# A fp32 trunk of two layers on one core: first loads cut in pieces and spread over two queues, zeros multiplied at the start, the pooling matrices outside the weight stream, and new distances in the list scheduler

## The chip, the cores and the metric

The kernel runs on one core of a Trainium2 chip. The metric is device time in microseconds, the median of several executions; below, one further execution taken by the hardware profiler is read. Engines: TensorE (PE, with PEld for its weight loads), VectorE (DVE), ScalarE (ACT), GpSimd (POOL) and SyncE (SP), whose queue issues the DMAs.

## What is computed

The reference is a causal trunk of two layers over 512 tokens of width 1024, all in float32. Each layer normalizes, projects once, and merges three mixers:

```python
h = rms_norm(x, norm_g[l])
p = h @ w_in[l]
(cb, cc, cx, cgate, q, k, v, agate, iq, ik, iw, pu, pgate, mgate) = split_columns(p)
y_a = short_conv_mixer(cb, cc, cx, cgate, ...)            # 3-tap causal convolution, gated
y_b = sparse_attention_mixer(q, k, v, agate, iq, ik, iw, ...)  # indexer scores, top-128 keys, softmax over them, 8 heads
y_c = pool_mixer(pu, pgate, pool_w[l], pool_scale[l], ...) # causal means of 2/4/8/16 tokens minus the token, times pool_w per group
g = sigmoid(mgate)                                         # three gates of width 1024
x = x + (g[0] * y_a + g[1] * y_b + g[2] * y_c) @ w_o[l]
```

The indexer scores of a query select the 128 highest keys; the softmax runs over those alone.

## The kernel before

The stream x is held transposed: eight slices `k` of 128 features by 512 tokens. Every matrix product is made of three matmuls in a reduced float32 format (`mm3`, L393): each operand is split into a high and a low part, and high x high, high x low and low x high are accumulated in PSUM. The split (`split`, L398) is a ScalarE copy for the high part and a VectorE subtraction for the low part. A 128-column group of a projection (`project`, L456) is 24 matmuls of 512 columns.

All weights come as one stream of chunks of 128 x 1024 (`wst`), 90 per layer. `prep` (L362) loads a chunk into `raw` (2 buffers), and splits it into `whi` and `wlo` (3 buffers each); `take` (L375) hands out the next one and prepares two more ahead. Chunk 0 is loaded and split in four pieces, chunks 1 and 2 in two, all others whole. One chunk of the stream, `pw`, is half empty and holds the pooling matrices; it is taken ahead of the pooling loop (L615) and its buffers stay in use until the fourth group is mixed (`mix`, L643).

At the start, SP issues all loads in turn: the vectors `vt`, the eight slices of x, and pieces of the first three chunks among them. `load_x` (L415) makes of each slice the scaled high and low parts `xhi` and `xlo` and a square, which POOL sums into `ss`. The first projections are a `wavefront` (L464) of three chunks over the slices as they arrive: `ps_ik`, `pa0`, `pb0`. Later come the indexer's scores (`select`, L556) and 16 rounds of `max` and `match_replace` for each of three token blocks (L576, L577), the pooling mixer, its merge (L591), the q and k projections of one quad of heads, v, attention for that quad (scores of a head and block in a bank `sc` of which there are 2; L724 is the first step of the softmax, on VectorE), the convolution, the second quad, and two more merges; `w_o` and the residual end the layer.

The order in which instructions stand on each engine is not that of the code. `Order` (L30) reads the recorded instructions and their dependences and plays them through a list scheduler with a cost for each (`cost`, L108); the first ready instruction of the highest priority is placed, four passes are made, and the best one's order on each engine is fixed. An instruction is ready for TensorE a distance `TO_PE` after the end of what it reads; a buffer comes free a distance `LAT` after the end of its last use:

```python
LAT = {"PE": 0.2, "DVE": 0.13, "Activation": 0.14, "Pool": 0.1, "SP": 0.13}
TO_PE = {"PE": 0.003, "DVE": 0.255, "Activation": 0.27, "Pool": 0.2, "SP": 0.27}

def lat(self, a, b):
    return self.TO_PE[a] if b == "PE" else self.LAT[a]
```

These numbers only set the order; on the chip an engine waits for what an instruction needs and for nothing else.

Of the kernel before, what the change touches and what calls it, by code (L numbers as in the profile page):

```python
# [5 lines left out]
F32 = mybir.dt.float32  # L6
F32R = mybir.dt.float32r
AF = mybir.ActivationFunctionType
# [3 lines left out]
LAG = 3  # L12
PASSES = 4
P = 128
S = 512
D = 1024
KT = D // P
DEPTH = 2
NCHUNK = 70 + 3 * 4 + 8
EPS = 1e-6  # L20
# [9 lines left out]
class Order:  # L30
# [6 lines left out]
    LAT = {"PE": 0.2, "DVE": 0.13, "Activation": 0.14, "Pool": 0.1, "SP": 0.13}  # L37
    TO_PE = {"PE": 0.003, "DVE": 0.255, "Activation": 0.27, "Pool": 0.2, "SP": 0.27}

# [68 lines left out]
    def cost(self, inst, kind):  # L108
# [14 lines left out]
        if kind == "InstMatmult":  # L123
            f32 = str(aps[0].dtype).endswith("float32")
            c = (0.0004167 * n + 0.003) * ((4 if n > 128 else 2) if f32 else 1)
            return c, 0.0
# [5 lines left out]
        if engine == "Pool":  # L132
            return (0.1 if kind == "InstMemset" else 0.1 + 0.0022 * n), 0.0
        if kind in ("InstMax", "InstMatchReplace"):
            return 0.069 + 0.00104 * max(size(a) for a in aps), 0.0
        fast = kind == "InstTensorScalarPtr" and len(wide) == 1 and not psum
# [165 lines left out]
@with_exitstack  # L302
def trunk(ctx, tc, xT, wst, vecs, cst, outT):
    nc = tc.nc
# [48 lines left out]

    def load(dst, src):
        nc.sync.dma_start(dst, src)  # L355

# [5 lines left out]
    def prep(i):  # L362
        l, c = divmod(i, NCHUNK)
        raw = wp.tile([P, 1024], F32, tag="raw", name=nm("raw"), bufs=2)
        hi = wp.tile([P, 1024], F32R, tag="whi", name=nm("whi"), bufs=3)
        lo = wp.tile([P, 1024], F32R, tag="wlo", name=nm("wlo"), bufs=3)
        n = 1024 // (4 if i == 0 else 2 if i < 3 else 1)
        for j in range(0, 1024, n):
            p = slice(j, j + n)
            load(raw[:, p], wst[l, c, :, p])  # L370
            act.activation(hi[:, p], raw[:, p], AF.Copy)  # L371
            dve.tensor_tensor(out=lo[:, p], in0=raw[:, p], in1=hi[:, p].bitcast(F32), op=ALU.subtract)  # L372
        wq[i] = (hi, lo)
# [66 lines left out]


    load(vt, vecs)
    for k in range(KT):
        if k in (0, 2, 4):
            prep(state["next"])
            state["next"] += 1
        if k % 4 == 0:
            xin = big(F32)
        load(xin[:, k % 4], xT[k])
        load_x(0, k, xin[:, k % 4])  # L450
# [24 lines left out]
    for l in range(DEPTH):  # L475
# [138 lines left out]

        pwh, pwl = take()  # L615
        yh, yl = big(), big()
# [217 lines left out]
def _columns():  # L834
# [13 lines left out]
    t += ab(iq, 0) + ab(iq, 1)  # L848
    t += ["pw"]
    for i in range(4):  # L850
# [13 lines left out]
def _layout(x, norm_g, w_in, conv_w, w_out_conv, q_norm_g, k_norm_g, w_out_attn, pool_w, pool_scale, w_out_pool, w_o):  # L864
# [4 lines left out]
    for l in range(DEPTH):  # L869
# [3 lines left out]
        for t in tiles:  # L873
            if isinstance(t, str) and t == "v":
                wst[l, n] = w[:, 2 * vc:2 * vc + 2, v0:v0 + S].reshape(P, 1024)
                vc += 1
                n += 1
            elif isinstance(t, str) and t == "pw":
                wst[l, n, :, :S] = pool_w[l].transpose(1, 0, 2).reshape(P, S)
                n += 1  # L880
            elif isinstance(t, str):
                br, wo = outs[t]
                wo = wo[l].reshape(4, P, KT, P).transpose(1, 2, 0, 3)
                for d in range(KT):
                    c = mg0 + br * D + d * P
                    wst[l, n] = w[:, :, c:c + P].reshape(P, 1024)
                    n += 1
                    if d % 2 == 1:
                        wst[l, n] = wo[:, d - 1:d + 1].reshape(P, 1024)
                        n += 1  # L890
            else:
                wst[l, n].reshape(P, KT, P)[:, :, :len(t)] = w[:, :, t]
                n += 1
# [13 lines left out]
    xT = np.ascontiguousarray(x[0].T.reshape(KT, P, S))  # L907
    return xT, wst, vecs

# [34 lines left out]
```

## Time and profile before

| | us |
|---|---|
| median of 3 runs (lowest, highest) | 1079.22 (1078.21, 1079.63) |
| the profiled execution, its own time | 1078.84 |
| its span, first to last instruction | 1077.1 |
| TensorE busy | 1065.4 |
| VectorE busy | 799.2 |
| ScalarE busy | 465.5 |
| first matmul starts | 6.51 |

The span is what the trace covers; the execution's own time is 1.7 us longer. Busy time of TensorE runs from a matmul's issue to its modelled end, so that consecutive ones overlap (390 ns each, started 227 ns apart); how fast they go is read from their starts.

### The profile page before, as it was taken

To read this page: it belongs to the slowest core of one execution; us is meant where nothing else is said; L and a number is where in the kernel's file an instruction comes from. 1 tells how busy PE (TensorE), PEld (TensorE's weight loads), DVE (VectorE), ACT (ScalarE), POOL (GpSimd) and SP (SyncE) were. 2 spreads that over 40 slices of the span, in tenths; PEclk is the share of its full clock that TensorE was granted. 3 is DMA by queue.
4 is the path that set the end of the run, shared out by engine and by line. 5 is a ranking of instruction groups with operands and counts; after the bars stand their busy time and mean duration, and the time that the engine had idled before them with its cause. 6 is when DMAs were issued, how large, how long until landed. Compare 5 with 4: busy or idle time off the path is not lost.

```text
span 1077.1 us, 13444 instructions
## 1 busy us (share of the span) xinstructions
PE 1065.4 (99%) x4842; PEld 878.4 (82%) x4842; DVE 799.2 (74%) x1389; ACT 465.5 (43%) x747; POOL 97.2 (9%) x76
## 2 busy tenths in 40 slices
PE   7999999999999999999999999999999999999998
PEld 6888888888888888888888888888888878888886
DVE  6889999997558865455559899999876598744442
ACT  6355233485233673233334542235852347623320
POOL 4000000000000011221210000000000001132210
PEclk9999999999999999999999999999999999999999
DMA  6542322452234522234535322225423245122352
GB/s 226 153 140 78 99 98 94 133 152 72 82 102 130 160 75 78 98 98 164 169 117 153 115 86 98 98 79 166 128 79 98 79 144 149 61 98 98 98 195 78
DMA packets 44402, 124.39 MB, mean 115 GB/s; under 512 B 6960, under 2 KB 7472, under 8 KB 44336
## 3 DMA queue, kind: packets, MB, share of 16 engines
q1 hardware_dynamic: 44336, 123.53, 36.4%
q8 instruction: 38, 0.62, 0.2%
q14 instruction: 28, 0.23, 0.1%
HBM read 101.49 MB, written 4.19 MB: 98 GB/s over the span
## 4 chain that ended last, share of the span: by engine, by line
PE 96%; DVE 1%; DMA 1%; issue 0%; ACT 0%; SPq 0%; DVEq 0%; ACTq 0%
PE pj L388 87%; PE sc L388 4%; PE pv L388 3%; PE pt L391 2%; DMA b<-in_x 0%; DVE wlo L372 0%; DMA k<-h 0%; DVE w L488 0%; SPq L355 0%; DVE h L401 0%; ACT whi L371 0%; DVE w L649 0%; ACT xhi L403 0%; DVE w L435 0%; DVE w L436 0%
## 5 line engine op out<-in xcount | busy, mean ns | idle before, releaser
L388 PE MATMUL pj<-xhi,whi 128*128 128x512 f32 x1040 | 373.1, 393 | 6.5 <-ACT whi L371 6.5
L388 PE MATMUL pj<-xlo,whi 128*128 128x512 f32 x1040 | 372.8, 393 | 0.0
L388 PE MATMUL pj<-xhi,wlo 128*128 128x512 f32 x1040 | 372.4, 393 | 0.0
L371 ACT ACTIVATE whi<-raw 128x1024 fp32r<-128x1024 f32 (+2 forms) x185 | 191.5, 1036 | 385.6 <-PE pj L388 358.9
L372 DVE TENSOR_TENSOR wlo<-raw,whi 128x1024 fp32r<-128x1024 f32 (+2 forms) x185 | 228.5, 1239 | 15.5 <-ACT whi L371 14.8
L388 PEld LDWEIGHTS pj<-xhi,whi 128*128 128x128 f32 x1040 | 195.0, 188 | 46.7 <-ACT whi L371 6.7
L388 PEld LDWEIGHTS pj<-xhi,wlo 128*128 128x128 f32 x1040 | 195.7, 188 | 39.4 <-DVE wlo L372 0.5
L388 PEld LDWEIGHTS pj<-xlo,whi 128*128 128x128 f32 x1040 | 195.5, 188 | 39.4
L388 PE MATMUL pj<-b,whi 128*128 128x512 f32 x640 | 210.7, 390 | 0.0
L385 DVE TENSOR_TENSOR w<-pj,ss 128x512 f32<-128x512 f32 x104 | 70.8, 684 | 93.3 <-PE pj L388 93.0
L388 PEld LDWEIGHTS pj<-b,whi 128*128 128x128 f32 x640 | 120.0, 188 | 24.2
L388 PE MATMUL pj<-b,wlo 128*128 128x512 f32 x320 | 118.2, 391 | 0.0
L610 POOL TENSOR_TENSOR b<-b,w 128x512 f32<-128x512 f32 x32 | 60.6, 1899 | 264.5 <-DVE w L608 264.4
L388 PEld LDWEIGHTS pj<-b,wlo 128*128 128x128 f32 x320 | 60.1, 188 | 12.3
L576 DVE MAX8 m<-score 128x8 f32<-128x256 f32 (+2 forms) x96 | 53.2, 557 | 1.7
L577 DVE MATCH_REPLACE8 score<-m,score 128x384 f32<-128x384 f32 (+2 forms) x96 | 52.0, 542 | 0.0
L742 DVE TENSOR_TENSOR pth<-pt,pth 128x128 fp32r<-128x128 f32 (+1 forms) x64 | 31.1, 486 | 18.7 <-PE pv L388 9.4
L819 DVE TENSOR_TENSOR w<-pj,w 128x512 f32<-128x512 f32 x16 | 11.0, 690 | 44.4 <-PE pj L388 42.8
L727 ACT ACTIVATE a<-a,mn 128x128 f32<-128x128 f32 (+1 forms) x64 | 35.6, 557 | 15.5 <-DVE mn L724 14.9
L665 POOL TENSOR_TENSOR w<-w,w 128x512 f32<-128x512 f32 x8 | 11.9, 1492 | 325.4 <-ACT w L664 325.4
L388 PE MATMUL pv<-pth,b 128*128 128x512 f32 (+3 forms) x128 | 39.9, 316 | 0.0
L741 ACT ACTIVATE pth<-pt 128x128 fp32r<-128x128 f32 (+1 forms) x64 | 27.6, 432 | 27.4 <-PE pt L391 20.1
(119 smaller groups left out, 999.7 us busy)
## 6 DMA issues: line engine op xcount, KB each, us to landing
raw<-in_w SPq DMA_DIRECT2D x177, 512.0 KB, 3.3
b<-h SPq DMA_DIRECT2D x128, 64.0 KB, 2.2
k<-h SPq DMA_DIRECT2D x64, 128.0 KB, 3.2
b<-in_x SPq DMA_DIRECT2D x8, 256.0 KB, 4.8
w<-in_x SPq DMA_DIRECT2D x8, 256.0 KB, 5.5
xs<-w SPq DMA_DIRECT2D x8, 256.0 KB, 2.3
w<-xs SPq DMA_DIRECT2D x8, 256.0 KB, 3.9
out_x<-w SPq DMA_DIRECT2D x8, 256.0 KB, 2.0
```

Source lines behind the costliest of these rows:

```text
L371: act.activation(hi[:, p], raw[:, p], AF.Copy)
L372: dve.tensor_tensor(out=lo[:, p], in0=raw[:, p], in1=hi[:, p].bitcast(F32), op=ALU.subtract)
L385: dve.tensor_tensor(out=out, in0=ps, in1=by, op=ALU.mult)
L388: pe.matmul(ps, lhs, rhs, start=start, stop=stop)
L391: pe.transpose(out, src, ident if n == P else ident[64:64 + n, 64:64 + n])
L576: dve.max(m8, score)
L577: dve.match_replace(score, m8, score, -3.0e38)
L610: gp.tensor_tensor(out=a, in0=a, in1=g, op=ALU.add)
L665: gp.tensor_tensor(out=s0, in0=s0, in1=s1, op=ALU.add)
L727: act.activation(pr[:, :w], pr[:, :w], AF.Exp, bias=mn, scale=-1.0, accum_out=zs)
L741: act.activation(dh, pst[:, :b + 1, :], AF.Copy)
L742: dve.tensor_tensor(out=dl, in0=pst[:, :b + 1, :], in1=dh.bitcast(F32), op=ALU.subtract)
```

## The change

The distances and three costs of the scheduler change; the first three chunks are loaded in pieces of 128, 128, 256 and 512 columns, each directly behind the x slice that needs it first, into tiles of the pool `b`; the first x slice is issued by ScalarE's queue instead of SP's; six matmuls of a zero tile into an unused PSUM bank stand at the start; all three first chunks are there before the loop ends; and the pooling matrices have an input and a load of their own, split into a tile of the pool `b`.

```diff
+WARM = 6
-NCHUNK = 70 + 3 * 4 + 8
+NCHUNK = 69 + 3 * 4 + 8
...
-    TO_PE = {"PE": 0.003, "DVE": 0.255, "Activation": 0.27, "Pool": 0.2, "SP": 0.27}
+    TO_PE = {"PE": 0.0, "DVE": 1.2, "Activation": 1.2, "Pool": 1.2, "SP": 2.0}
...
-            c = (0.0004167 * n + 0.003) * ((4 if n > 128 else 2) if f32 else 1)
+            c = (0.000423 * n + 0.01) * ((4 if n > 128 else 2) if f32 else 1)
...
-            return (0.1 if kind == "InstMemset" else 0.1 + 0.0022 * n), 0.0
+            return (0.1 if kind == "InstMemset" else 0.1 + 0.003 * n), 0.0
         if kind in ("InstMax", "InstMatchReplace"):
-            return 0.069 + 0.00104 * max(size(a) for a in aps), 0.0
+            n = max(size(a) for a in aps)
+            return 0.069 + 0.00104 * n + 0.076 * (kind == "InstMatchReplace"), 0.0
...
-    def load(dst, src):
-        nc.sync.dma_start(dst, src)
+    def load(dst, src, queue=nc.sync):
+        queue.dma_start(dst, src)
...
-        n = 1024 // (4 if i == 0 else 2 if i < 3 else 1)
-        for j in range(0, 1024, n):
-            p = slice(j, j + n)
-            load(raw[:, p], wst[l, c, :, p])
-            act.activation(hi[:, p], raw[:, p], AF.Copy)
-            dve.tensor_tensor(out=lo[:, p], in0=raw[:, p], in1=hi[:, p].bitcast(F32), op=ALU.subtract)
+        load(raw, wst[l, c])
+        split(hi, lo, raw)
...
-    load(vt, vecs)
+    idle = W(F32R)
+    gp.memset(idle.bitcast(F32), 0.0)
+    warm = pt()
+    for n in range(WARM):
+        mm(warm.rearrange("p a b -> p (a b)"), idle[:, :P], idle, n == 0, n == WARM - 1)
+    HEAD = 3
+    raws = [big(F32).rearrange("p (a b) s -> p a (b s)", a=2) for _ in range(2)]
+    heads = []
+    for i in range(HEAD):
+        hi = wp.tile([P, 1024], F32R, tag="whi", name=nm("whi"), bufs=3)
+        lo = wp.tile([P, 1024], F32R, tag="wlo", name=nm("wlo"), bufs=3)
+        wq[i] = (hi, lo)
+        heads.append((raws[i // 2][:, i % 2], hi, lo))
+    state["next"] = HEAD
+    piece = {0: 1, 1: 1, 2: 2, 4: 4}
     for k in range(KT):
-        if k in (0, 2, 4):
-            prep(state["next"])
-            state["next"] += 1
         if k % 4 == 0:
             xin = big(F32)
-        load(xin[:, k % 4], xT[k])
+        load(xin[:, k % 4], xT[k], nc.scalar if k == 0 else nc.sync)
+        for i, (raw, hi, lo) in enumerate(heads if k in piece else ()):
+            p = slice(k * P, (k + piece[k]) * P)
+            load(raw[:, p], wst[0, i, :, p])
+            split(hi[:, p], lo[:, p], raw[:, p])
+            if k == 0 and i == 0:
+                load(vt, vecs)
         load_x(0, k, xin[:, k % 4])
...
-        pwh, pwl = take()
+        pw = big()
+        pwh, pwl = pw[:, 0], pw[:, 1]
+        pwr = W()
+        load(pwr, pws[l])
+        split(pwh, pwl, pwr)
```

The rest of the diff makes the new input `pws` and leaves the chunk `pw` out of the stream.

ScalarE at the start. Before (`whi_84` and `whi_117` are the first two chunks, `xhi_100` to `xhi_126` slices of x):

```order
L423 ACT_TABLE_LOAD
L423 ACTIVATE a_104<-b_98 128x512
L403 ACTIVATE xhi_100<-b_98,vt 128x512
L403 ACTIVATE xhi_109<-b_98,vt 128x512
L371 ACTIVATE whi_84<-raw_83 128x256
L423 ACTIVATE a_113<-b_98 128x512
L371 ACTIVATE whi_117<-raw_116 128x512
L403 ACTIVATE xhi_126<-b_98,vt 128x512
```

Now (`whi_93`, `whi_95`, `whi_97` are the first three chunks):

```order
L357 DMA b_99<-in_x 128x512
L421 ACT_TABLE_LOAD
L421 ACTIVATE a_115<-b_99 128x512
L401 ACTIVATE xhi_111<-b_99,vt 128x512
L398 ACTIVATE whi_93<-b_91 128x128
L398 ACTIVATE whi_95<-b_91 128x128
L398 ACTIVATE whi_97<-b_92 128x128
L401 ACTIVATE xhi_129<-b_99,vt 128x512
L398 ACTIVATE whi_93<-b_91 128x128
L421 ACTIVATE a_133<-b_99 128x512
L398 ACTIVATE whi_95<-b_91 128x128
```

The second slice's copy moved from ahead of the first piece of weights to behind three of them, and further on four squares (`a_133`, `a_150`, `a_158`, `a_176`) stand behind the first one and ahead of the last slice's copy. On TensorE the six matmuls of zeros come first, and then each slice of x is multiplied with all three chunks before the next, nine matmuls a slice, where before the first two chunks alternated and the third followed.

TensorE at the end of the first three chunks, now (`xhi_196` is the last slice's high part, `whi_207` and `whi_213` are the fourth and fifth chunk):

```order
L386 MATMUL pj_218<-xhi_196,wlo_94 128x512
L386 MATMUL pj_219<-xhi_196,whi_95 128x512
L386 MATMUL pj_219<-xlo_197,whi_95 128x512
L386 MATMUL pj_219<-xhi_196,wlo_96 128x512
L386 MATMUL pj_220<-xhi_196,whi_97 128x512
L386 MATMUL pj_220<-xlo_197,whi_97 128x512
L386 MATMUL pj_220<-xhi_196,wlo_98 128x512
L386 MATMUL pj_353<-xhi_111,whi_207 128x512
L386 MATMUL pj_353<-xlo_112,whi_207 128x512
L386 MATMUL pj_408<-xhi_111,whi_213 128x512
L386 MATMUL pj_408<-xlo_112,whi_213 128x512
L386 MATMUL pj_353<-xhi_111,wlo_208 128x512
```

Before, the third chunk's matmuls stood between the first chunk's last use and the fourth chunk's first:

```order
L388 MATMUL pj_198<-xhi_176,wlo_85 128x512
L388 MATMUL pj_200<-xlo_101,whi_142 128x512
L388 MATMUL pj_199<-xhi_176,whi_117 128x512
L388 MATMUL pj_200<-xhi_100,wlo_143 128x512
L388 MATMUL pj_199<-xlo_177,whi_117 128x512
L388 MATMUL pj_200<-xhi_109,whi_142 128x512
L388 MATMUL pj_199<-xhi_176,wlo_118 128x512
L388 MATMUL pj_200<-xlo_110,whi_142 128x512
L388 MATMUL pj_200<-xhi_109,wlo_143 128x512
L388 MATMUL pj_200<-xhi_126,whi_142 128x512
L388 MATMUL pj_333<-xhi_100,whi_187 128x512
L388 MATMUL pj_200<-xlo_127,whi_142 128x512
```

What moved is again the third chunk (`pj_200`): its 24 matmuls no longer stand ahead of and between the fourth chunk's.

VectorE at the first softmax of layer 1 (L576 and L577 are steps of the top-k, L724 the softmax's first step). Before, the last top-k steps stand among the first softmax operations:

```order
L385 TENSOR_TENSOR w_1944<-pj_1919,ss_106 128x512
L576 MAX m_210_874<-score_461 128x8
L724 ISA a_1988,mn_1989<-sc_1985,ct 128x128
L724 ISA mn_1989 128x1
L577 MATCH_REPLACE score_461<-m_210_874,score_461 128x512
L724 ISA a_1999,mn_2000<-sc_1996,score_459 128x256
L724 ISA mn_2000 128x1
L576 MAX m_211_877<-score_461 128x8
L724 ISA a_2010,mn_2011<-sc_2007,score_460 128x384
L724 ISA mn_2011 128x1
L577 MATCH_REPLACE score_461<-m_211_877,score_461 128x512
```

Now all of them, with the scaling of the mask (L594), the splits of v (L730) and two evictions (L383), stand ahead of the first softmax operation (L744):

```order
L593 MATCH_REPLACE score_481<-m_211_896,score_481 128x512
L730 SCALAR_TENSOR_TENSOR b_1922<-pv_1800,rcol_467,b_1922 128x8x64
L594 TENSOR_SCALAR score_481<-score_481 128x512
L399 TENSOR_TENSOR wlo_1970<-raw_1968,whi_1969 128x1024
L730 SCALAR_TENSOR_TENSOR b_1921<-pj_1798,rcol_467,b_1921 128x8x64
L730 SCALAR_TENSOR_TENSOR b_1922<-pj_1799,rcol_467,b_1922 128x8x64
L383 TENSOR_TENSOR w_1963<-pj_1938,ss_117 128x512
L383 TENSOR_TENSOR w_1999<-pj_1974,ss_117 128x512
L744 ISA a_2007,mn_2008<-sc_2004,ct 128x128
L744 ISA mn_2008 128x1
L744 ISA a_2018,mn_2019<-sc_2015,score_479 128x256
```

What moved are three steps of the top-k and the operations around them, from behind the first softmax operation to ahead of it.

## Rows read from the trace of the kernel before

**Rows 1.** The page: busy time of an engine, share of the span, instructions.
```profile
PE 1065.4 (99%) x4842; PEld 878.4 (82%) x4842; DVE 799.2 (74%) x1389; ACT 465.5 (43%) x747; POOL 97.2 (9%) x76
```

**Rows 2.** Chain that ended last, pieces: start us, us, what, number of instructions.
```profile
6.51 25.90 PE pj L388 x101
...
403.21 0.33 PE pt L391 x3
...
409.82 154.21 PE pj L388 x680
...
1073.31 0.69 DVE w L819
```

**Rows 3.** TensorE by shape: first and last 512-column group, largest 128-column one.
```profile
L388 PE MATMUL pj<-xhi,whi 128*128 128x512 f32 x1040 | 373.1, 393 | 6.5 <-ACT whi L371 6.5
...
L391 PE MATMUL pt<-ct,a 128*128 128x128 f32 x160 | 28.0, 273 | 0.2
...
L388 PE MATMUL sc<-h,wlo 128*128 128x512 f32 x8 | 3.1, 390 | 0.0
```

**Rows 4.** TensorE at the start: windows (busy, granted clock, DMA), then order of time.
```profile
9.00:11.00 2.00, 2.00 (x7) 1.00 1.03 364
...
10.52 1.05 PE L388 MATMUL pj<-xhi,whi 128*128 128x512 f32 x2
...
11.37 0.97 PE L388 MATMUL pj<-xlo,whi 128*128 128x512 f32 x2
```

**Rows 5.** TensorE in attention stretches: order of time, then one window of four.
```profile
901.10 0.63 PE L388 MATMUL pj<-b,whi 128*128 128x512 f32 x2
...
902.73 0.40 PE L388 MATMUL pj<-b,whi 128*128 128x512 f32 x1
...
205.00:265.00 60.00, 60.00 (x298) 1.00 0.41 120
```

**Rows 6.** TensorE in order of time: the three waits that are named.
```profile
361.45 0.69 PE L388 MATMUL sc<-k,b 128*128 128x128 f32 x4 [0.25 <-DMA k<-h]
...
605.38 0.39 PE L388 MATMUL sc<-b,b 128*128 128x256 f32 x1 [0.61 <-DVE w L649]
...
874.09 0.50 PE L388 MATMUL sc<-w,ob 128*128 128x512 f32 x1 [0.31 <-DVE w L401]
```

**Rows 7.** All engines in order of time: from the first load to the first matmul.
```profile
0.74 0.39 SPq L355 DMA_DIRECT2D b<-in_x  x1
...
3.44 0.63 ACT L423 ACTIVATE a<-b 128x512 f32<-128x512 f32 x1 [1.42 <-DMA b<-in_x]
...
3.97 0.70 ACT L403 ACTIVATE xhi<-b,vt 128x512 fp32r<-128x512 f32 x1
...
4.71 0.75 DVE L404 SCALAR_TENSOR_TENSOR xlo<-b,vt,xhi 128x512 fp32r<-128x512 f32 x1 [4.71 <-ACT xhi L403]
...
6.06 0.40 ACT L371 ACTIVATE whi<-raw 128x256 fp32r<-128x256 f32 x1
...
6.51 0.80 PE L388 MATMUL pj<-xhi,whi 128*128 128x512 f32 x1 [6.51 <-ACT whi L371]
```

**Rows 8.** VectorE and POOL in order of time: splits beside additions of squares.
```profile
13.99 8.37 POOL L428 TENSOR_TENSOR ss<-ss,a 128x512 f32<-128x512 f32 x5 [1.21 <-ACT a L423]
...
14.57 1.53 DVE L372 TENSOR_TENSOR wlo<-raw,whi 128x256 fp32r<-128x256 f32 x1
...
16.02 1.78 DVE L404 SCALAR_TENSOR_TENSOR xlo<-b,vt,xhi 128x512 fp32r<-128x512 f32 x1
```

**Rows 9.** The page: the weight split, busy us, mean ns, idle before and releaser.
```profile
L371 ACT ACTIVATE whi<-raw 128x1024 fp32r<-128x1024 f32 (+2 forms) x185 | 191.5, 1036 | 385.6 <-PE pj L388 358.9
...
L372 DVE TENSOR_TENSOR wlo<-raw,whi 128x1024 fp32r<-128x1024 f32 (+2 forms) x185 | 228.5, 1239 | 15.5 <-ACT whi L371 14.8
```

**Rows 10.** VectorE: a top-k step in order of time; busy time from 70 to 218.
```profile
217.65 0.68 DVE L576 MAX8 m<-score 128x8 f32<-128x512 f32 x1
...
sum 148.00, DVE 143.19; mean DVE 17.90
```

More of the change, by code (lines that the diff above doesn't have):

```diff
@@ L302, in trunk @@
 @with_exitstack
-def trunk(ctx, tc, xT, wst, vecs, cst, outT):
+def trunk(ctx, tc, xT, wst, pws, vecs, cst, outT):
     nc = tc.nc
@@ L848, in _columns @@
     t += ab(iq, 0) + ab(iq, 1)
-    t += ["pw"]
     for i in range(4):
@@ L876, in _layout @@
                 vc += 1
-                n += 1
-            elif isinstance(t, str) and t == "pw":
-                wst[l, n, :, :S] = pool_w[l].transpose(1, 0, 2).reshape(P, S)
                 n += 1
@@ L907, in _layout @@
     xT = np.ascontiguousarray(x[0].T.reshape(KT, P, S))
-    return xT, wst, vecs
+    pws = np.ascontiguousarray(pool_w.transpose(0, 2, 1, 3).reshape(DEPTH, P, S))
+    return xT, wst, pws, vecs
 def _constants():
@@ L932 @@
     from concourse.bass_utils import run_bass_kernel_spmd
-    xT, wst, vecs = _layout(**{k: np.asarray(v) for k, v in inputs.items()})
-    arrays = {"in_x": xT, "in_w": wst, "in_v": vecs, "in_c": _constants()}
+    xT, wst, pws, vecs = _layout(**{k: np.asarray(v) for k, v in inputs.items()})
+    arrays = {"in_x": xT, "in_w": wst, "in_p": pws, "in_v": vecs, "in_c": _constants()}
     nc = bacc.Bacc("TRN2", target_bir_lowering=False, num_devices=1)
```

## Prediction

> **What bounds the kernel now.** I read the shares of the engines first: TensorE is busy for 1065.4 of 1077.1 us [rows 1]. A kernel like that gains only what TensorE loses, so the next views are those that say where it loses. The chain of work that ended last has long pieces in which nothing is lost: 680 matmuls in 154.21 us, 0.2268 us each, which is the steady price of a 512-column matmul here [rows 2]. Three 128-column transposes take 0.33 us, 0.11 each [rows 2]. The view by shape gives the number of each: the 17 groups of 512 columns hold 4412 matmuls (first and last shown), 128 columns 232, and there are 96 each of 384 and 256 and 6 of 8 columns [rows 3]. In steady state they need 4412 x 0.2268 + 96 x (0.170 + 0.113) + 238 x 0.11 = 1054 us (the middle prices in proportion to columns). The first starts at 6.51 and the last ends by 1073.3, where the final VectorE addition starts [rows 2]. So 1073.3 - 6.5 - 1054 = 12.8 us are lost between them, besides the 6.5 before and 3.8 behind. The tail's code and order do not change.
>
> Of the 12.8, the chain's first piece has 101 matmuls in 25.90 us, which is 3.0 over their 22.9 [rows 2]. The reason is in the order of time: from 10.52 to 11.37 two 512-column matmuls start in 0.85 us, half the steady rate, 512 columns at 1.2 GHz [rows 4]. The granted clock reads 1.00 (2.4 GHz) in that stretch although only 7 matmuls ran in 2 us [rows 4]; I go by the spacing. TensorE had been at work since 6.51 and rose to the upper level at about 12.1, 5.6 us after its first matmul.
>
> The other 9.8 us lie in the selection and attention stretches. There 512-column matmuls that wait for nothing start 0.233 us apart (seven starts from 901.10 to 902.73, [rows 5]); there are four attention stretches of this kind, one of them with 298 matmuls in 60 us [rows 5], so some 1200 less the 430 narrow ones, and 770 x 0.006 would be up to 5 us of slower streaming, which no distance of waits removes. That leaves about 4.8 us of waits. The three named ones are 0.61, 0.31 and 0.25 us [rows 6].
>
> **The change, part by part.**
>
> *First data.* Before, the first x lands and ScalarE starts on it at 3.44; square (0.53 to the next start), scaled copy, then weights, with a second x tile ahead of them; TensorE starts at 6.51 [rows 7]. Now ScalarE does square, copy, and at once a 128-column piece. From 3.44: 0.53 + about 0.70 for the copy = 4.67, plus 0.3 for the piece (between 0.2 and the 0.40 of the 256-column one [rows 7]) makes 5.0. If the pieces in the other queue delay x (92 KB in front of or among its 256 KB, whose landing took 2.7 us from issue), add up to 0.4: 5.0 to 5.4.
>
> The first x is now issued by ScalarE while SP issues vectors and weights; an issue takes 0.39 us [rows 7], so between 0 and 0.4 us comes from the second queue, and I have taken none. The Trainium skill (DMA: Bandwidth & Descriptors, Issuing engines are not separate DMA queues) says that queues of different engines share the same 16 DMA engines and that a second issuer saves only issue time. By it, too, the sum would stay within 0.4 us of mine; if instead two queues doubled the rate, x would land up to a microsecond earlier. No run so far shows two queues.
>
> SP now issues 19 transfers up to the last x slice; at 0.39 to 0.45 each that one leaves by about 9.3, and ScalarE reaches it after 14. The constants moved behind the fourth and fifth chunk on SP; VectorE first reads them behind the head, near 22. Both are hidden: 0. Without that cover a late slice would cost TensorE its delay in full.
>
> *The zeros.* Six matmuls of zeros at the lower level take 6 x 0.427 = 2.6 us, from about 1.3 (after a POOL fill of one tile) to 3.9, in time where TensorE idles anyway: price nothing, and if the fill were late they would push the first real one at most by what lies past 5.0. What they can return is the 3.0 us of the head.
>
> *The head, limited by splitting.* All three weight chunks are now multiplied per slice of x: 72 matmuls, 16.3 us at the steady price, so 21.3 if nothing waits. VectorE has 8 low parts of x at 0.75 [rows 7], and 3 x 1.24 for the weights [rows 9] in 12 pieces, about 0.7 more for the cuts: 10.4 us. While POOL adds squares, a 256-column piece took 1.53 and an x part 1.78 [rows 8], about 1.0 longer; four such additions stand ahead of the last x slice in ScalarE's new order: +4. VectorE starts at 4.71 and is through between 19.1 (no wait) and 21 (two for data); eight matmuls (1.8 us) follow the last slice's low part. The head ends between 21.3 and 22.8: 0 to 1.5 lost, I take 0.8.
>
> *A new wait behind it.* All three high buffers belong to the head until its last slice. The fourth chunk's copy waits for the first chunk's last matmul, only six matmuls (1.4 us) before the head's end, and takes 1.04 [rows 9]; the fifth's copy and the fourth's low part (1.24) come behind it, and TensorE has two matmuls of cover, where before it had the third chunk's 24, nine ahead of it and the rest among it. Price 0.6 to 1.5, I take 1.0.
>
> Head in all: before, 6.5 + 3.0 = 9.5; after, 5.0 + 0.8 + 1.0 = 6.8: **-2.7 us**, between -3.9 (5.0, 0, 0.6) and -1.1 (5.4, 1.5, 1.5).
>
> *pool_w apart.* Per layer half a ScalarE copy (0.5) and half a VectorE subtraction (0.6) go, and half a load; the matrix no longer holds one of three weight buffers during the pooling stage. TensorE waits for no weights there now, so: 0.
>
> *Longer distances.* The table now plans 1.2 us instead of 0.255 from VectorE to a matmul, and 2.0 instead of 0.27 from a DMA. The growth, 0.945 and 1.73, is longer than each wait seen. But it covers data alone: the 0.31 (data from VectorE) and the 0.25 (a DMA). A buffer that comes free is still planned at 0.13, and that is the 0.61 wait (a score bank behind L649). So 0.56 of 1.17 named, half; of 4.8 us I take half, **-2.5 us**, between 0 and -4.8.
>
> *Order of streams.* With the distance between matmuls at 0, TensorE finishes one chunk before it turns to another, where before two alternated. Alternation cost nothing in the steady piece (0.2268 with it), so 0; if the slower 0.233 came from it, another 2 to 5 us would go.
>
> Sum: -5.2 us. The profiled execution took 1078.84 (its span and 1.7 around it), 0.4 below the median of 1079.22; the forecast against that median is **1074.0**.
>
> **The rivals.** *Only the head gains.* The planned distances fall into time where TensorE had other work or move the waits to buffers. For it: the largest wait seen is of that kind. 1079.2 - 2.7 = 1076.5.
>
> *The zeros do not do their work.* The clock rises 5.6 us after the first real matmul, at 10.6. Until then 13 matmuls at 0.427 instead of 0.2268 cost 2.6, less the 0.8 of slack counted above: +1.8, so 1075.8, or 1078.3 if the distances bring nothing either. For it: the zeros end about 1 us before data comes. By the Trainium skill (TensorE: Matmul & The Clock Gate, Part 1) activity releases the gate and idling closes it, so the gap after the zeros may forfeit part of their work; no run yet shows which.
>
> *Top-k comes late: slower.* The order now puts the last three top-k steps and four more operations ahead of the first softmax on VectorE: 3 x 0.68 [rows 10], a scaling 0.34, a further eviction and a value split of about 0.7 each, 3.8 us. From 70 to 218 us VectorE is busy 143.2 of 148 [rows 10], so 4.8 are free; if these cannot be used, because they are scattered behind TensorE and ScalarE, the third score waits, twice (each layer once). It decides from the point where less than 3.8 of the 4.8 can be used; at the full price, and the distances' gain lost to it, 1079.2 - 2.7 + 7.6 = 1084.1. Against it: before, the same chain reached 218.25 with no wait on TensorE.
>
> *Streaming was slowed by alternation.* 1069 to 1072.
>
> **How the numbers follow.** A measurement of this kernel can tell about 0.2%, 2.2 us, from no change. Forecast 0.6 (its own range 1071.3 to 1076.6 from the bounds of its two terms); only the head 0.17; zeros without effect 0.1; top-k late 0.06, which with half its price is near no change; alternation 0.07. The range takes all but the extremes: 1070.8 to 1077.9. Faster by over 0.2% (below 1077.0): the forecast, alternation, two thirds of only the head and half of the clock case, 0.82; within: 0.13; slower 0.05.
>
> **What would show it.** First real matmul at 5.0 to 5.4; spacing 0.227 from the first slices on, or 0.427 until 10.6 if the zeros fail; TensorE waiting about 1 us for the fourth chunk's copy near 21 to 23; 101 steady matmuls' worth of work done 2 to 3 us earlier. The waits at the second key quad and at the normalization gone, the one for a score bank kept. Wrong if TensorE waits at the first scores near 214, if the head's matmuls wait for low parts for more than 2 us, or if the loss outside the head stays at 9.8.

## The result and the profile after

| | before | after |
|---|---|---|
| median (lowest, highest), 4 runs each | 1079.43 (1078.21, 1080.31) | 1092.5 (1091.03, 1093.75) |
| ratio, 95% interval | 1 | 1.0122 [1.0109, 1.0134] |
| the profiled execution, its own time | 1078.84 | 1093.75 |
| its span | 1077.1 | 1092.0 |

The change makes the kernel 13 us slower; forecast were 5 us less. The page of the changed kernel: busy time of the engines (share of the span, instructions), then the chain that ended last, by engine.

```profile
PE 1072.7 (98%) x4848; PEld 875.5 (80%) x4848; DVE 803.3 (74%) x1393; ACT 459.2 (42%) x751; POOL 86.5 (8%) x77
...
PE 78%; DVE 10%; DMA 3%; issue 3%; ACT 3%; SPq 2%; POOL 0%; DVEq 0%; ACTq 0%; POOLq 0%
```

The busy line hides the loss, for the reason given with the times before: a matmul's busy time runs to its modelled end, and short gaps hide in it. The chain tells more: before, TensorE held 96% of it, with pieces as long as the 680 matmuls of [rows 2]; now 78%. The rest goes through VectorE, ScalarE and the DMAs, so TensorE waits for helpers all along.

To place the loss I took the starts of all matmuls and took off the steady price of each (0.2266 us for 512 columns, 0.1735 for 384, 0.1175 for 256, 0.109 for 128 or fewer, all from undisturbed starts). Between 25 us and the last matmul the kernel before loses 10.1 us and the changed one 26.7: +16.6. The steady stretches are as fast as before. The loss is spread over some twenty places. Of the 26.7, 12.9 are waits that the profile names (1.2 of the 10.1 before); the rest are later starts too short for a name, among them some 0.1 us at the second matmul behind each wait. The waits that TensorE has by name (line, releaser, us in total, times, longest us):

```profile
PE sc L386 <- DVE mn L744: 2.5, 4, 0.9
PE sc L386 <- ACT a L582: 2.2, 2, 1.7
PE pt L389 <- DVE rz L749: 1.4, 2, 0.8
PE pt L386 <- POOL z L643: 1.3, 1, 1.3
PE sc L386 <- ACT w L398: 1.3, 2, 0.6
PE pt L389 <- DVE w L545: 1.3, 1, 1.3
PE pj L386 <- DVE w L502: 1.2, 2, 0.6
PE pj L386 <- ACT w L495: 1.1, 2, 0.6
...
PE pt L389 <- DVE pth L762: 0.8, 4, 0.2
```

Before, besides the start, three waits of 1.2 us in all stood here [rows 6]. The 1.3 us for POOL are the start: the zeros wait for their tile. Of the others the larger half are not for data (7.7 of 12.9 us). `mn` (L744), `a` (L582), `w` (L495, L502) and `pth` (L762) are operations that read a PSUM bank, and the matmul behind them wants the bank, not the result. Here is one in order of time (start us, us, engine, line, op, tile; in brackets the idle time and its releaser), at the first attention of a quad:

```profile
367.20 0.39 PE L386 MATMUL pj<-xhi,wlo 128*128 128x512 f32 x1
367.53 0.68 DVE L383 TENSOR_TENSOR w<-pj,ss 128x512 f32<-128x512 f32 x1
368.13 0.28 DVE L744 CUSTOM_DVE_ANT_0 a<-sc,ct 128x128 f32<-128x128 f32 x1
...
368.47 1.08 PE L386 MATMUL sc<-k,b 128*128 128x384 f32 x4 [0.88 <-DVE mn L744]
```

The first softmax step stands on VectorE behind an eviction and other work, so it reads its score bank late, and TensorE, which wants one of the two `sc` banks for the next score, stands for 0.88 us. Another place shows a queue held by a transfer:

```profile
66.66 8.04 SPq L357 DMA_DIRECT2D raw<-in_w  x3
...
70.83 1.06 ACT L398 ACTIVATE whi<-raw 128x1024 fp32r<-128x1024 f32 x1 [1.96 <-DMA raw<-in_w]
71.79 0.37 ACT L582 ACTIVATE a<-sc 128x256 f32<-128x256 f32 x1
...
72.21 0.74 PE L386 MATMUL sc<-b,b 128*128 128x256 f32 x4 [1.74 <-ACT a L582]
```

ScalarE waits 1.96 us for a chunk of weights; the copy that would empty a score bank stands behind it, and TensorE pays 1.74.

The start, TensorE alone in order of time:

```profile
1.31 2.93 PE L386 MATMUL pt<-w 128*128 128x512 f32 x6 [1.31 <-POOL z L643]
5.27 1.22 PE L386 MATMUL pj<-xhi,whi 128*128 128x512 f32 x2 [1.03 <-ACT whi L398]
...
8.42 0.49 PE L386 MATMUL pj<-xlo,whi 128*128 128x512 f32 x1
8.75 0.39 PE L386 MATMUL pj<-xhi,wlo 128*128 128x512 f32 x1
...
16.88 0.50 PE L386 MATMUL pj<-xhi,wlo 128*128 128x512 f32 x1 [0.30 <-DVE wlo L399]
...
25.32 0.50 PE L386 MATMUL pj<-xhi,whi 128*128 128x512 f32 x1 [0.54 <-ACT w L495]
```

The first matmul of data moved from 6.51 [rows 7] to 5.27, the full rate from 12.18 to 8.75; behind the half rate of [rows 4] the order of time before goes on with

```profile
12.18 0.63 PE L388 MATMUL pj<-xhi,wlo 128*128 128x512 f32 x2
```

Two new waits follow in the changed kernel. Taking off the price of the matmuls done, 26 us into the program the kernel before is 9.36 us behind a TensorE that had run from 0 on, and the changed one 8.67: the head gives 0.7 us, not 2.7. (The wait at 25.32 counts in this and in the 26.7; from 26 us on the changed kernel loses 25.9.)

### The profile page after: what moved, and what is told of

Read it like the earlier page. It is cut to its first block, busy times and chain, and to the rows that moved or that the text cites. A ratio compares the mean times of both kernels' runs of the same rounds, so it can differ in the third digit from the quotient of the medians.

```text
span 1092.0 us, 13469 instructions
## 1 busy us (share of the span) xinstructions
PE 1072.7 (98%) x4848; PEld 875.5 (80%) x4848; DVE 803.3 (74%) x1393; ACT 459.2 (42%) x751; POOL 86.5 (8%) x77
## 4 chain that ended last, share of the span: by engine, by line
PE 78%; DVE 10%; DMA 3%; issue 3%; ACT 3%; SPq 2%; POOL 0%; DVEq 0%; ACTq 0%; POOLq 0%
PE pj L386 70%; PE sc L386 4%; DVE wlo L399 3%; PE pv L386 2%; DMA raw<-in_w 2%; SPq L357 2%; PE pt L389 2%; ACT whi L398 1%; DMA b<-h 1%; DVE w L504 1%; DVE w L383 1%; POOL w L685 0%; DVE m L592 0%; DVE w L502 0%; DMA b<-in_x 0%
## 5 line engine op out<-in xcount | busy, mean ns | idle before, releaser
L386 PE MATMUL pj<-xhi,whi 128*128 128x512 f32 x1040 | 408.2, 393 | 3.3 <-DVE w L502 1.2
L386 PE MATMUL pj<-xlo,whi 128*128 128x512 f32 x1040 | 408.2, 392 | 0.0
L386 PE MATMUL pj<-xhi,wlo 128*128 128x512 f32 x1040 | 407.2, 392 | 0.3 <-DVE wlo L399 0.3
L398 ACT ACTIVATE whi<-raw 128x1024 fp32r<-128x1024 f32 x175 | 184.8, 1058 | 377.8 <-PE pj L386 301.7
L399 DVE TENSOR_TENSOR wlo<-raw,whi 128x1024 fp32r<-128x1024 f32 x175 | 227.8, 1304 | 36.1 <-ACT whi L398 32.6
L386 PE MATMUL pj<-b,whi 128*128 128x512 f32 x640 | 198.0, 390 | 0.0
L383 DVE TENSOR_TENSOR w<-pj,ss 128x512 f32<-128x512 f32 x104 | 71.0, 686 | 91.7 <-PE pj L386 91.2
L626 POOL TENSOR_TENSOR b<-b,w 128x512 f32<-128x512 f32 x32 | 45.6, 1426 | 280.3 <-DVE w L624 280.3
L593 DVE MATCH_REPLACE8 score<-m,score 128x256 f32<-128x256 f32 (+2 forms) x96 | 52.0, 543 | 0.0
L762 DVE TENSOR_TENSOR pth<-pt,pth 128x128 fp32r<-128x128 f32 (+1 forms) x64 | 31.1, 486 | 20.8 <-ACT pth L761 20.3
L624 DVE SCALAR_TENSOR_TENSOR w<-w,pj 128x512 f32<-128x512 f32 x32 | 21.9, 685 | 32.5 <-ACT b L401 16.8
L398 ACT ACTIVATE h<-w 128x512 fp32r<-128x512 f32 (+1 forms) x36 | 22.3, 628 | 43.3 <-DVE w L505 22.3
```

The lines of the kernel that those rows point to most:

```text
L383: dve.tensor_tensor(out=out, in0=ps, in1=by, op=ALU.mult)
L386: pe.matmul(ps, lhs, rhs, start=start, stop=stop)
L398: act.activation(hi, src, AF.Copy)
L399: dve.tensor_tensor(out=lo, in0=src, in1=hi.bitcast(F32), op=ALU.subtract)
L593: dve.match_replace(score, m8, score, -3.0e38)
L624: dve.scalar_tensor_tensor(a if first else g, g, 1.0, py, op0=ALU.add, op1=ALU.mult)
```

## The experiments

Theory A: the scheduler's numbers make the loss, either by the distance 0 between matmuls (A1) or by the long distances to TensorE (A2). Theory B: the new loads and pool_w apart make it. Times are medians; the ratio is to the kernel before, measured beside each, whose median lay between 1078.76 and 1079.17.

**Old numbers, new loads (e1).** The changed kernel with

```diff
-    TO_PE = {"PE": 0.0, "DVE": 1.2, "Activation": 1.2, "Pool": 1.2, "SP": 2.0}
+    TO_PE = {"PE": 0.003, "DVE": 0.255, "Activation": 0.27, "Pool": 0.2, "SP": 0.27}
```

and the three old costs (the diff of the change, backwards).

> The changed kernel with the scheduler's old distances and costs: new first loads, zeros, and pooling matrices apart. Theory A (the loss comes from the new scheduler numbers, and the head gained what its trace shows, about 1.5 us): 1076.5 to 1079. Theory B (the new loads or the pooling matrices apart make the loss): 1088 or more.

Measured 1084.78, ratio 1.0053 [1.0038, 1.0068]. Most of the loss is gone, so A holds for the larger part; but 5.6 us stay, which neither theory had.

**New numbers, old loads (e2).** The kernel before with the new costs and

```diff
-    TO_PE = {"PE": 0.003, "DVE": 0.255, "Activation": 0.27, "Pool": 0.2, "SP": 0.27}
+    TO_PE = {"PE": 0.0, "DVE": 1.2, "Activation": 1.2, "Pool": 1.2, "SP": 2.0}
```

> The kernel before with the scheduler's new distances and costs alone. Theory A: 1092 to 1096, the changed kernel's loss without its head. Theory B: 1077 to 1080.

Measured 1093.15, ratio 1.0127 [1.0112, 1.0142]. The numbers alone make a loss as large as the whole. TensorE's named waits in it (after the 5.0 us of the start) are again led by banks:

```profile
PE sc L389 <- DVE mn L725: 3.5, 4, 1.1
PE sc L389 <- ACT a L567: 2.5, 2, 1.3
PE pt L392 <- DVE pth L743: 1.1, 6, 0.2
PE pt L392 <- DVE w L530: 1.1, 1, 1.1
```

**The distance between matmuls (e3, e4).** e3 is the changed kernel, e4 the kernel before, each with the other's number.

```diff
-    TO_PE = {"PE": 0.0, "DVE": 1.2, "Activation": 1.2, "Pool": 1.2, "SP": 2.0}
+    TO_PE = {"PE": 0.003, "DVE": 1.2, "Activation": 1.2, "Pool": 1.2, "SP": 2.0}
```
```diff
-    TO_PE = {"PE": 0.003, "DVE": 0.255, "Activation": 0.27, "Pool": 0.2, "SP": 0.27}
+    TO_PE = {"PE": 0.0, "DVE": 0.255, "Activation": 0.27, "Pool": 0.2, "SP": 0.27}
```

> The changed kernel with the distance between matmuls back at 0.003, the long distances kept. Theory A1 (distance 0 makes TensorE stay with one accumulator, and that makes the waits): accumulators alternate again and the time falls to 1074 to 1079. Theory A2 (the long distances from the other engines make the waits): it stays within 3 us of 1092.5, alternating or not.

Measured 1089.06, ratio 1.0094 [1.0077, 1.0110].

> The kernel before with the distance between matmuls at 0 and nothing else changed. Theory A1: 1088 to 1095, with accumulators one after the other. Theory A2: within 2 us of 1079.4.

Measured 1082.27, ratio 1.0028 [1.0017, 1.0039]. The edit does what it seems to: the accumulator changes between one matmul and the next 4593 times before, 703 times in e4, 721 in the changed kernel, 4658 in e3. It is worth 3 us in either place, a little more than A2 allowed (within 3 us of 1092.5, within 2 of 1079.4): A1 is no main cause.

**Long distances alone (e5).** The kernel before, with old costs and

```diff
-    TO_PE = {"PE": 0.003, "DVE": 0.255, "Activation": 0.27, "Pool": 0.2, "SP": 0.27}
+    TO_PE = {"PE": 0.003, "DVE": 1.2, "Activation": 1.2, "Pool": 1.2, "SP": 2.0}
```

> The kernel before with one line changed: the distances to TensorE of the four other engines are 1.2, 1.2, 1.2 and 2.0 us, TensorE's own stays 0.003, the old costs stay. Theory L (the long distances by themselves make the loss): 1087 to 1095 us, as the kernel before with all the new numbers had (1093.2). Theory C (the new costs make it, the distances matter little): 1078 to 1083 us.

Measured 1089.07, ratio 1.0091 [1.0074, 1.0107]: +10, as theory L had it. Half of that, though, lies in one stretch (5.2 us from 575 to 600, where the kernel before loses 0.5), which asks how much of such a number belongs to the edit.

**Banks (e9).** e2 with a long release for PSUM banks:

```diff
+rel = self.lat(e, "PE") if self.slot[name][0] in ("pj", "sc", "pt", "pv") else self.LAT[e]
-heapq.heappush(releases, (last[name] + self.LAT[e], self.slot[name][0], i))
+heapq.heappush(releases, (last[name] + rel, self.slot[name][0], i))
```

> The kernel before with all the new numbers (1093.2 us), and one more line: the release of a PSUM bank is given the same long distance to TensorE as data, where it had 0.13 us. Theory R (TensorE waits now for banks, because the plan leaves 1.2 us for data and 0.13 us for a bank that the same engines give back): the waits for bank releases (nearly all of the 9.5 us of named waits behind the first load) go, 1076 to 1084 us. Theory P (the loss comes from the order of the work on VectorE and ScalarE, since a due time 1 us earlier for all that feeds TensorE puts it ahead of other links of the chains): 1088 to 1096 us.

Measured 1086.53, ratio 1.0072 [1.0057, 1.0087]: 6.6 of the 14 us come back, between the theories. The waits of `mn` and `a` fell from 6.0 us to 0.2; what is left behind the start is of other kinds:

```profile
PE sc L390 <- ACT h L402: 1.9, 2, 1.0
PE pt L393 <- DVE pth L744: 1.5, 2, 0.9
PE pt L393 <- DVE w L531: 1.1, 1, 1.1
```

So banks planned at 0.13 us while data has 1.2 are a part of the loss, not all of it. With margins of 1.2 us on data and banks alike, this plan is still 7.8 us behind.

**Each part of the loads alone (e10, e11).** e10 is the kernel before with the part of the change's diff from `def load` to `load_x(0, k, ...)`, e11 with the part on `pwh, pwl` and `NCHUNK`. All numbers are old.

> The kernel before with the new first loads and the zeros alone; pool_w stays in the stream of weights, all numbers of the scheduler stay. Theory H (the head brings what its own stretch shows, 0.8 to 1.5 us, and nothing else moves): 1077.5 to 1079 us. Theory S (the new loads shift everything behind them, and the changed kernel with the old numbers lost its 5.6 us by them): 1082 to 1086 us.

Measured 1084.77, ratio 1.0053 [1.0038, 1.0068].

> The kernel before with pool_w loaded on its own, outside the stream of weights; the first loads and all numbers stay. Theory H' (pool_w apart cost the 5.6 us of the changed kernel with the old numbers, since two more big tiles and a load in the middle of the pooling branch stand in the way): 1082 to 1087 us. Theory S: 1078.5 to 1080.5 us, as before.

Measured 1082.99, ratio 1.0037 [1.0023, 1.0051]. Each alone is slower by 4 to 6 us, and both together (e1) by no more: not a sum of costs. In e10, ScalarE stands for a transfer, as above (ScalarE and TensorE in order of time):

```profile
47.39 0.63 ACT L397 ACTIVATE h<-w 32x512 fp32r<-32x512 f32 x1 [9.52 <-DMA b<-h]
47.92 0.16 ACT L560 ACTIVATE iw<-pt 128x24 f32<-128x24 f32 x1
...
48.14 0.55 PE L388 MATMUL pt<-ct,ss 128*128 128x128 f32 x3 [1.50 <-ACT iw L560]
```

A split that waits 9.52 us for a move was put ahead of the 0.16 us copy that frees the only `pt` bank. That is an accident of the order, and no part of the edit asks for it. So on the chip an instruction waits not only for what it needs itself, as was said of the order above, but also for what stands ahead of it in its engine's queue.

**Null edits (n1, n3).** The kernel before, n1 with the first and n3 with the second line:

```diff
-    TO_PE = {"PE": 0.003, "DVE": 0.255, "Activation": 0.27, "Pool": 0.2, "SP": 0.27}
+    TO_PE = {"PE": 0.003, "DVE": 0.26, "Activation": 0.27, "Pool": 0.2, "SP": 0.27}
...
+    TO_PE = {"PE": 0.003, "DVE": 0.23, "Activation": 0.25, "Pool": 0.2, "SP": 0.27}
```

> A null edit: the kernel before with VectorE's distance to TensorE 0.260 us in place of 0.255. No wait can need these 5 ns, but the plan is drawn anew, and most instructions of TensorE come in another place. Theory N (the plan of the kernel before is a lucky draw, any new draw costs some us, and so do the new loads, pool_w apart and the distance 0): 1081 to 1086 us. Theory Q (these edits cost what they cost by themselves, a new draw alone costs nothing): 1078 to 1080 us.

Measured 1082.89, ratio 1.0033 [1.0021, 1.0044].

> A second null edit: the kernel before with the distances of VectorE and ScalarE to TensorE 0.23 and 0.25 us in place of 0.255 and 0.27. Theory N: 1081 to 1086 us. Theory Q: 1078 to 1080.5 us.

Measured 1082.02, ratio 1.0027 [1.0017, 1.0036]. Five nanoseconds in a table cost 3.8 us: theory N. The plan of the kernel before is better than both, so a plan drawn anew can be 3 to 4 us behind with no cause of its own, and e4, e10 and e11 lie within 3 us of these nulls. Nothing can be said of them one by one. Two nulls do not show that every new draw starts that far behind; m4, m6 and m7 below do not.

**Due times (p1).** e2, but the due times of the other engines' work are worked out with the old distances (`NEED`).

```diff
-                s = [need[j] - self.lat(e, ops[j]["e"])
+                s = [need[j] - (self.NEED if ops[j]["e"] == "PE" else self.LAT)[e]
```

> The kernel before with all the new numbers (1093.2 us), but the due times are worked out with the old distances; the long ones hold only in the play, where they say when a matmul may start. Theory P (the harm comes from due times 1 us earlier for all that feeds TensorE): 1079 to 1085 us. Theory R (it comes from the play, which moves the matmul that waits for data back and lets others take the banks): 1089 to 1096 us.

Measured 1093.7, ratio 1.0135 [1.0120, 1.0150]: theory P falls: old distances in the due times give nothing back. The due times of p1 still hold the new costs, so for those the run leaves open whether they act there or in the play.

**Costs alone (e6), and split (m1, m2).** e6 has the three new costs and the old distances; m1 the matmul's alone, the first pair of lines; m2 the other two, of which POOL's is shown.

```diff
-            c = (0.0004167 * n + 0.003) * ((4 if n > 128 else 2) if f32 else 1)
+            c = (0.000423 * n + 0.01) * ((4 if n > 128 else 2) if f32 else 1)
...
-            return (0.1 if kind == "InstMemset" else 0.1 + 0.0022 * n), 0.0
+            return (0.1 if kind == "InstMemset" else 0.1 + 0.003 * n), 0.0
```

> The kernel before with the new costs alone (matmul, POOL, MATCH_REPLACE8), the old distances. With the long distances alone at 1089.1 us and both at 1093.2 us, a sum of two effects gives 1082 to 1084 us here. If the new costs, which are nearer to the trace, help where the distances are short: 1076 to 1079 us.

Measured 1091.65, ratio 1.0117 [1.0100, 1.0134]: outside both ranges, nearly the whole loss without any long distance.

> The kernel before with the matmul's new cost alone (0.2266 us for 512 columns, as the trace has it, in place of 0.2163). Theory M (the old cost, 5% under the trace, was a margin: a plan drawn with a TensorE that is too fast has the other engines ahead of it on the chip; with the true cost they come just in time and every delay that the plan doesn't know is a wait): 1088 to 1094 us. Theory O (the costs of POOL and MATCH_REPLACE8 move the other engines' work, the matmul's cost only scales the plan): 1080 to 1085 us, a new draw.

Measured 1096.79, ratio 1.0164 [1.0149, 1.0179]: this one line makes the kernel before 17.7 us slower, more than the whole change. Its waits, after the 6.3 us of the start:

```profile
PE sc L388 <- ACT w L400: 4.8, 4, 1.8
PE pj L388 <- DVE wlo L372: 1.7, 3, 0.7
PE pj L388 <- DVE z L385: 1.5, 1, 1.5
PE pj L388 <- DVE b L710: 1.3, 2, 1.0
```

> The kernel before with the new costs of POOL's additions and of MATCH_REPLACE8 alone. Theory M: 1080 to 1085 us, a new draw. Theory O: 1088 to 1094 us.

Measured 1085.56, ratio 1.0057 [1.0041, 1.0072]: 0.6 over the range of M, 2.7 and 3.5 us above the two nulls, and far under theory O.

**A cost that is more wrong (m3).**

```diff
-            c = (0.0004167 * n + 0.003) * ((4 if n > 128 else 2) if f32 else 1)
+            c = (0.00039 * n + 0.003) * ((4 if n > 128 else 2) if f32 else 1)
```

> The kernel before with a matmul cost that is wrong by twice as much (0.2027 us for 512 columns, 10% under the trace). Theory M (a margin): no slower than a new draw, 1077 to 1083 us, with fewer named waits on TensorE than with the new costs. Theory O, or a best value in between: 1084 to 1092 us.

Measured 1084.27, ratio 1.0042 [1.0028, 1.0056], a little over the range of M, at the lower end of the other. It is a draw like the others; 7.6 of its losses lie in one stretch, 750 to 800. So 10% under the trace lies among the draws at 5%, 1 to 2 us above the nulls, while the trace's own price is slower in each of the pairs that differ in that line alone: by 17.7 us (m1 and before), 6.1 (e6 and m2) and 12 (the changed kernel and m4, below). M stands as far as the trace's own price goes; whether a best value lies between is not shown. The same line also moves the plan's 128-column transposes, from 0.113 to 0.128 us (0.109 in the trace); that part was not tried apart from the wide matmuls.

**The one line put back (m4).** The changed kernel with

```diff
-            c = (0.000423 * n + 0.01) * ((4 if n > 128 else 2) if f32 else 1)
+            c = (0.0004167 * n + 0.003) * ((4 if n > 128 else 2) if f32 else 1)
```

> The changed kernel with one line put back: the matmul's old cost (0.2163 us for 512 columns, 5% under the trace); long distances, distance 0, the other new costs, the new loads and pool_w apart all stay. Theory M (the lost margin of the matmul's cost is the larger part, the long distances cover data but no banks and add some): 1084 to 1089 us, with fewer than 60 of the 130 sc banks taken again within 0.3 us of their release (80 in the changed kernel, 40 in the kernel before). Theory L (the long distances harm whatever the cost is): 1090 to 1095 us.

Measured 1080.54, ratio 1.0012 [1.0002, 1.0022]: 12 of the 13 us are back, 3.5 under the range of M. 46 `sc` banks are taken again within 0.3 us. Its page, the same two lines as above:

```profile
PE 1068.6 (99%) x4848; PEld 880.9 (82%) x4848; DVE 801.0 (74%) x1393; ACT 458.0 (42%) x751; POOL 81.9 (8%) x77
...
PE 85%; DVE 7%; issue 3%; DMA 3%; ACT 2%; SPq 1%; DVEq 0%; ACTq 0%
```

**Toward a better version (m6, m7).** m6 is the changed kernel with the old costs, the line of e9 for banks and the first line here; m7 is m4 with the second, used for banks as in e9.

```diff
+    TO_PE = {"PE": 0.003, "DVE": 0.5, "Activation": 0.5, "Pool": 0.4, "SP": 0.5}
...
+rel = 0.5 if self.slot[name][0] in ("pj", "sc", "pt", "pv") else self.LAT[e]
```

> The changed kernel's loads and pool_w apart, the old costs, TensorE's distance 0.003, and distances of 0.5 us for data from VectorE and ScalarE (twice the old ones), with the same 0.5 us for the release of a PSUM bank. If a margin that covers data and banks alike is what the plan lacked: 1075 to 1080 us, at or under the kernel before. If any redrawn plan costs its 3 us and the margin adds nothing: 1081 to 1085 us, as the changed kernel with all the old numbers (1084.8).

Measured 1078.78, ratio 0.9999 [0.9990, 1.0009].

> The changed kernel with the matmul's old cost (1080.5 us), and the release of a PSUM bank at 0.5 us in place of 0.13. If the banks that are taken again at once (46 of the 130 sc banks within 0.3 us there) still cost something: 1075 to 1079 us, under the kernel before. If what is left comes from a new draw and from data and loads: 1080 to 1084 us.

Measured 1079.86, ratio 1.0005 [0.9996, 1.0014], between its two ranges. Both are level with the kernel before; no version beat it. m6 lies in the range that stood for a margin on data and banks alike. m6 is 6 us faster than e1, which has the same loads and the old distances; m7 and m4 cannot be told apart.

**All twenty programs side by side.** From each trace, with the order of its program laid beside it, I took two things: how many of the 130 uses of an `sc` bank begin within 0.3 us of the end of the release they need (the n-th use against the release two earlier, in order of time), and the median time from the end of an attention split `pth` to the first matmul that reads it.

| program | distances to TensorE | us | `sc` within 0.3 us | `pth` lead, us |
|---|---|---|---|---|
| matmul planned 5% under the trace | | | | |
| before | old | 1079.1 | 40 | 0.37 |
| n1, n3 (nulls) | old | 1082.9, 1082.0 | 41, 42 | 0.44, 0.36 |
| e4, e11 | old | 1082.3, 1083.0 | 42, 33 | 0.36, 0.36 |
| e1, e10, m2 | old | 1084.8, 1084.8, 1085.6 | 49, 53, 37 | 0.36, 0.49, 0.36 |
| e5 | long | 1089.1 | 55 | 1.42 |
| m4 | long | 1080.5 | 46 | 1.50 |
| m6, m7 | 0.5, long; banks 0.5 | 1078.8, 1079.9 | 3, 8 | 0.58, 1.44 |
| planned 10% under it (m3) | old | 1084.3 | 27 | 0.57 |
| planned as in the trace | | | | |
| m1, e6 | old | 1096.8, 1091.7 | 71, 64 | 0.23, 0.30 |
| after, e2, p1 | long | 1092.5, 1093.2, 1093.7 | 80, 80, 80 | 1.24, 1.26, 1.25 |
| e3 | long | 1089.1 | 76 | 1.24 |
| e9 | long, banks long | 1086.5 | 12 | 1.25 |

Of the seven programs with the true price none is under 1086.5; of the thirteen others one is over it.

## Why the prediction was wrong

**The step that failed.** The prediction lists the change part by part, and the new cost of a matmul is in no part. It was taken as a number that only sets the order, and stands at nothing without a reason. By m1 that line is worth +17.7 us, by e6 and m2 6.1, and by m4 it is 12 of the 13 us. It has no wait of its own to be priced by: it takes a margin from every chain. With a TensorE that is planned 5% too fast, whatever other engines must do between two matmuls has 5% more time on the chip than in the plan. With the true price the plan has results and banks come just in time, and what it doesn't know can become a wait: a split beside POOL that takes longer, a move that lands late, a queue that stands. The table shows this for old distances: `pth` leads of 0.57, 0.37 and 0.23 us and 27, 40 and 71 tight banks, for 10%, 5% and 0% (m3, before, m1), while the nulls stay at 0.36 to 0.44 and 41 to 42.

VectorE shows it too. In the stretch from 100 to 190 us, which the top-k fills, its busy time (window, length, busy) is, before:

```profile
100.00:190.00 90.00, 86.42 (x182) 1.00 0.30 100
```

in m1, planned at the true price:

```profile
100.00:190.00 90.00, 87.11 (x188) 1.00 0.30 100
```

and in m3, at 10% under it:

```profile
100.00:190.00 90.00, 82.34 (x171) 1.00 0.31 100
```

The slower the planned TensorE, the more operations are packed onto VectorE in the same time: 188, 182, 171, with 2.9, 3.6 and 7.7 us idle. The changed kernel and m4, which differ in this line alone, show the same, 3.0 and 5.8 us idle:

```profile
100.00:190.00 90.00, 87.04 (x185) 1.00 0.30 94
...
100.00:190.00 90.00, 84.19 (x180) 1.00 0.30 94
```

That the line makes the loss is shown by the three pairs. The way from it to each wait is argued: that this packing, rather than the banks, is how the margin is lost was not tried alone, and e9, whose VectorE is as full (87.37), is 6.6 us faster than e2.

**"Longer distances, -2.5 us."** The mechanism did what the step says: `pth` leads grew from 0.37 to 1.24 us, and the caveat named there, that a bank is still planned at 0.13, became the rule: 80 tight banks for 40. Nor did the distances hold for data on the chip: the wait at the normalization, 0.31 us in one layer before [rows 6], is 0.64 now in each (`sc` for `w`, L398). Of the three waits named before, that for the move is gone. But the sum took half of 4.8 us as gained and set no price on the loss. Alone, the distances gave +10 (e5); with the other new costs, distance 0 and the loads, but the old matmul price, +1.4 (m4). No program with them beat the kernel before. With draws apart by several us, whether they gain or cost by themselves is open: m4 has them and is 4.2 us faster than e1, which has the same loads and all the old numbers.

**"Order of streams, 0."** e4 is 3.2 us slower, like a null, so 0 stands. The rival that alternation slowed the streaming falls: in the attention stretch from 225 to 250 us, where the starts of [rows 5] are slightly apart, 43 matmuls before and 49 after, now without alternation, start 0.003 to 0.03 us late, with 0.29 and 0.33 us in all.

**"Head, -2.7 us."** Its first step held: 5.27 lies in 5.0 to 5.4. The second queue brought nothing: the first x reached ScalarE at 3.78, where it was 3.44 [rows 7].

```profile
0.73 0.41 ACTq L357 DMA_DIRECT2D b<-in_x  x1
...
3.78 0.63 ACT L421 ACTIVATE a<-b 128x512 f32<-128x512 f32 x1 [1.32 <-DMA b<-in_x]
```

The Trainium skill (DMA: Bandwidth & Descriptors, Issuing engines are not separate DMA queues) says that a second issuer is no second set of DMA engines; by that rule no earlier landing was to be had, and the trace agrees, with 3.78 for 3.44. The zeros were credited with all 3.0 us. The changed kernel did reach the full rate 3.48 us after its first data, where the kernel before took 5.67, but that is no effect of theirs that the runs can show: the other six programs with the same zeros took 4.78 to 5.67 us, and the twelve others without them 3.55 to 7.81. In m4 the half rate holds to 10.46, as without zeros:

```profile
10.04 0.63 PE L386 MATMUL pj<-xhi,wlo 128*128 128x512 f32 x1
10.46 0.46 PE L386 MATMUL pj<-xhi,whi 128*128 128x512 f32 x1
10.77 0.39 PE L386 MATMUL pj<-xlo,whi 128*128 128x512 f32 x1
```

So the rival in which the zeros don't do their work was the better account of that term, though in the changed kernel itself the rate rose at 8.75, before the 10.6 of that rival. A program without the zeros and all else equal was not run. The wait for the fourth chunk, 1.0 us near 21 to 23, did not come; waits of 0.30 at a low part and 0.54 at an eviction came in its place.

**"pool_w apart, 0."** e11 is a draw like n1, so 0 is not contradicted.

**"Top-k comes late."** The steps stand ahead of the first softmax as the order shows, but the last step of the top-k starts at 214.4 (before 220.6), and the first softmax step is through 0.7 us after the first score's start, before 0.9; in the second layer the last step of the top-k starts at 752.6, 5.6 us ahead of the first score. The rival did not happen. What did happen is on the side it stood for, a plan whose helpers are late for TensorE, but in twenty places and by another line. The sign "the loss outside the head stays at 9.8" was the right alarm, and it went to 26.7.

**The chances.** 0.05 for slower was too little also for a reason that no row of before shows: both null edits made the plan 3 to 4 us slower for nothing. An edit that redraws a plan should allow for that. The forecast's own range, 1071.3 to 1076.6, is also narrower than its bounds make it: -8.7 to -1.1 us from 1079.2 is 1070.5 to 1078.1.

## What to carry to other kernels

A number in a planner is part of the plan's margin, whatever it is named. A cost corrected to the trace can take away slack that hid what the planner does not model. Whether explicit margins can stand in for it is open here: 1.2 us on data and banks beside the true price (e9) left 7.8 us of loss, 0.5 us on both beside the old price (m6) was level with the kernel before. Before reading a difference of a few us between two plans, run several null edits, such as 5 ns in a distance, to learn how much a new draw is worth. And look at in-order queues: an instruction that waits for a DMA holds the short one behind it that TensorE needs.

## What was not expected of the hardware

Wide matmuls start 0.43 us apart at first and 0.227 later, about what 512 columns take at TensorE's levels of 1.2 and 2.4 GHz. The rise came between 3.5 and 7.8 us after the first matmul of data in these twenty programs, with waits of at most some 1 us in between. Programs with the same zeros and nearly the same first matmul differ by 2 us in it (8.75 in the changed kernel, 10.77 in m4). The granted clock of these windows reads 1.00 at the half rate too, in the changed kernel as before:

```profile
5.00:7.00 2.00, 1.73 (x4) 1.41 (x5) 1.44 (x5) 1.56 (x7) 0.08 (x1) 1.00 0.91 292
```

This is a window of the changed kernel: length, then busy time and instructions of PE, PEld, DVE, ACT and POOL, granted clock, DMA share and GB/s. Its four matmuls start 0.59 and then 0.43 us apart, the half rate, beside a clock of 1.00.
